# Another order for the seven products of an up-projection pair, with its releases, result split and token sums moved

## The chip, the cores and the metric

The kernel runs on one core of one Trainium2 chip. The metric is the device time of one execution in microseconds (us), the median of three runs. A core has a matrix engine, TensorE (PE, with its weight loads PEld), and three engines for elementwise work: VectorE (DVE), ScalarE (ACT) and GpSimd (POOL). SyncE (SP) issues transfers. Each engine takes its own instructions in order and waits on semaphores for the others.

## The reference

The reference is one inference step of a four-stage streaming trunk over 576 tokens of width 1024 (512 of a new stream, 64 of a running one). Each sublayer's result goes through `x <- LayerNorm(ALPHA * x + sublayer(x))`:

```
x = layer_norm(ALPHA * x + attention(x))      # chunked band attention, 16 heads
x = layer_norm(ALPHA * x + mlp_0(x))
x = layer_norm(ALPHA * x + ssm(x))            # Mamba-2 scan with convolution
x = layer_norm(ALPHA * x + mlp_1(x))
mlp(x) = square(relu(x @ W_up)) @ W_down      # 1024 -> 4096 -> 1024
```

The change touches the two MLPs alone, and in them the up-projection `square(relu(x @ W_up))`.

## The kernel before, in words

Activations lie with features on the 128 partitions and the 576 tokens in the free dimension, in two halves of 288 (T1, T2). Float32 precision comes from splitting each operand into a high part rounded for TensorE and the low rest (`xh`, `xl` for the activations, `wh`, `wl` for the weights); a product is the sum of three matmuls, high by high, high by low and low by high. A weight slab of 128x1024 is loaded by SP into `wr`, rounded on ACT into `wh` (L171), and the rest is computed on DVE into `wl` (L173).

The up-projection of an MLP has 32 tiles of 128 output features. The first four are done plainly, half by half of the tokens (`first_tiles`, matmuls L324), while the LayerNorm of the second half and the token sums run as side work between the matmuls; their relu and square are L465 and L466, the split of the result L467 and L468. The other 28 tiles of a layer go in 14 pairs (`up_pair`, matmuls L514): two weight slabs, two halves of the inner dimension and two halves of the tokens make a two-by-two block product, which seven products of blocks give in place of eight. A product is 12 matmuls of 128x288 over four blocks of 128. The names b11, b21 and b22 stand for plain activation blocks, t1 to t4 for sums of blocks. The token sums for t1 to t4 are formed once per MLP (L481, L485, L489, L496 on DVE, then `combine`: the rounding L471 on ACT and the rest L472 on DVE). The weight sums are formed per pair by four POOL operations (L187, L190, L191, L192) on the raw slabs, between the splits.

A pair holds two PSUM tiles, `ab` and `cd`, with two halves each (a, b, c, d). The results are put together in SBUF in `ut` (four rows of 288): ACT copies a finished half into it (L526, L532, L536), and DVE adds others (L524; the last add takes both halves of `cd` as 576 columns). Then ACT does relu and square over 1152 columns (L546, L547), and DVE splits the result (hh L549, hl L550). The down-projection (matmuls L294 `mm<-hh,...`) reads hh and hl; its result is added to x by L368 and L370.

The order per layer is MLP_ORDER (L68): first tiles, 3 pairs, down 0, 4 pairs, down 1, 4 pairs, down 2, 3 pairs, down 3. Each of the downs 0 to 2 is preceded by one pair that belongs to the next. Within this, a tile scheduler places the instructions on each engine's queue, so that the queues are not simply the order of the source; `W.get`, `W.load` and `W.drop` say when a weight set is formed and when its buffer may be used again.

## Time and profile before

| | |
|---|---|
| median of three runs | 1772.41 us (1769.83 to 1773.49) |
| profiled execution | 1774.35 us, its span 1772.6 us |
| PE busy | 1683.3 us, 95% |
| DVE busy | 1090.8 us, 62% |
| ACT busy | 744.1 us, 42% |
| POOL busy | 445.0 us, 25% |
| mean granted clock of PE | 0.98 |

The durations below come from the profiled execution. The span is the time from its first to its last instruction. Idle time of an engine costs something only where a chain of waits ends at PE, which is busy nearly throughout. In a timeline row the bracket gives the idle time of the engine before the instruction and what ended it; `x2` joins consecutive instructions of one form, and the duration is then that of all.

### The profile page before, as it was taken

The page shows a single profiled execution, that of the slowest core. Times are in us where ns is not written, and L with a number is a line of the kernel's source. Part 1 is how long each engine was busy: PE and PEld are TensorE (multiplying, and loading weights), DVE is VectorE, ACT ScalarE, POOL GpSimd, SP SyncE. Part 2 cuts the span into 40 slices and gives each one's busy share as a digit, 9 for nine tenths or more (in the row PEclk, how much of TensorE's full clock was granted, in tenths as well). Part 3 has the DMA queues.
Part 4 walks back from the last instruction along what each step waited for, and adds up shares of the span by engine and source line. Part 5 has one row for each costly group of instructions (what it writes and reads, how often), then busy time and mean ns, then how long its engine had stood idle before and what let it go on. Part 6 is the DMA issues. An engine that isn't in the chain of part 4 may idle for free.

```text
span 1772.6 us, 30745 instructions
## 1 busy us (share of the span) xinstructions
PE 1683.3 (95%) x12521; PEld 1592.3 (90%) x12521; DVE 1090.8 (62%) x1874; ACT 744.1 (42%) x1182; POOL 445.0 (25%) x449
## 2 busy tenths in 40 slices
PE   9999999789999999989999999999988999999995
PEld 8888888779989899989899999999877998999995
DVE  5555555885463635387776776777878636354445
ACT  5434432453241524255663563556235515243332
POOL 0000002421211312335541341334351112130211
PEclk9999999989999999999999999999988999999997
DMA  7343331113131322213432332333110313213121
GB/s 261 101 128 101 111 106 55 48 48 119 48 119 48 96 83 84 84 51 116 122 104 81 96 104 85 109 99 107 56 48 24 120 48 104 76 60 119 49 72 54
DMA packets 76924, 157.20 MB, mean 89 GB/s; under 512 B 11440, under 2 KB 40240, under 8 KB 76784
## 3 DMA queue, kind: packets, MB, share of 16 engines
q1 hardware_dynamic: 76784, 155.25, 27.5%
q8 instruction: 98, 1.61, 0.4%
q14 instruction: 42, 0.34, 0.1%
HBM read 145.80 MB, written 9.42 MB: 88 GB/s over the span
## 4 chain that ended last, share of the span: by engine, by line
PE 80%; DVE 10%; POOL 3%; ACT 3%; issue 2%; DMA 1%; SPq 0%; DVEq 0%; ACTq 0%; POOLq 0%
PE mm L294 51%; PE mm L514 12%; PE mm L324 3%; DVE wl L173 2%; PE ax L748 1%; PE mm L303 1%; ACT wh L171 1%; PE ax L1053 1%; PE ax L770 1%; PE ax L1056 1%; DVE tmp L398 1%; PE ax L719 1%; PE ax L358 1%; PE ax L1058 1%; DVE hl L550 1%
## 5 line engine op out<-in xcount | busy, mean ns | idle before, releaser
L171 ACT CAST wh<-wr 128x1024 fp32r<-128x1024 f32 (+1 forms) x279 | 279.4, 1006 | 508.0 <-PE mm L294 363.7
L173 DVE TENSOR_TENSOR wl<-wr,wh 128x1024 fp32r<-128x1024 f32 (+1 forms) x258 | 322.7, 1252 | 95.5 <-ACT wh L171 91.9
L294 PE MATMUL mm<-xh,wl 128*128 128x288 f32 x1056 | 231.6, 300 | 0.0
L294 PE MATMUL mm<-xh,wh 128*128 128x288 f32 x1056 | 230.8, 300 | 0.1
L294 PE MATMUL mm<-xl,wh 128*128 128x288 f32 x1056 | 230.8, 299 | 0.0
L294 PE MATMUL mm<-hh,wl 128*128 128x288 f32 x960 | 223.3, 298 | 0.0
L294 PE MATMUL mm<-hl,wh 128*128 128x288 f32 x960 | 223.0, 298 | 0.0
L294 PE MATMUL mm<-hh,wh 128*128 128x288 f32 x960 | 223.0, 298 | 0.0
L370 DVE TENSOR_TENSOR x<-x,mm 128x288 f32<-128x288 f32 (+1 forms) x112 | 64.7, 581 | 209.9 <-PE mm L294 198.8
L294 PEld LDWEIGHTS mm<-xl,wh 128*128 128x128 f32 x1056 | 169.3, 189 | 4.1 <-issue 3.8
L294 PEld LDWEIGHTS mm<-xh,wh 128*128 128x128 f32 x1056 | 169.7, 189 | 2.4 <-issue 1.4
L294 PEld LDWEIGHTS mm<-xh,wl 128*128 128x128 f32 x1056 | 169.6, 189 | 1.6
L294 PEld LDWEIGHTS mm<-hh,wl 128*128 128x128 f32 x960 | 161.4, 190 | 0.1
L294 PEld LDWEIGHTS mm<-hh,wh 128*128 128x128 f32 x960 | 161.3, 190 | 0.1
L294 PEld LDWEIGHTS mm<-hl,wh 128*128 128x128 f32 x960 | 161.2, 190 | 0.0
L514 PE MATMUL mm<-th,wh 128*128 128x288 f32 x336 | 106.3, 316 | 33.1 <-DVE ut L524 23.5
L514 PE MATMUL mm<-xh,wh 128*128 128x288 f32 x448 | 136.5, 305 | 0.6 <-ACT ut L532 0.6
L514 PE MATMUL mm<-xl,wh 128*128 128x288 f32 x448 | 133.5, 298 | 0.3 <-DVE xl L472 0.3
L514 PE MATMUL mm<-xh,wl 128*128 128x288 f32 x448 | 133.3, 298 | 0.0
L187 POOL TENSOR_TENSOR wr<-wr 128x512 f32<-128x512 f32 x28 | 42.0, 1500 | 342.8 <-DMA wr<-in_wts 322.4
L514 PEld LDWEIGHTS mm<-th,wh 128*128 128x128 f32 x336 | 63.7, 189 | 44.6 <-DVE ut L524 33.7
L514 PE MATMUL mm<-tl,wh 128*128 128x288 f32 x336 | 99.7, 297 | 0.0
(255 smaller groups left out, 3598.1 us busy)
## 6 DMA issues: line engine op xcount, KB each, us to landing
wr<-in_wts SPq DMA_DIRECT2D x223, 512.0 KB, 3.4
cumb<-cumd SPq DMA_DIRECT2D x32, 256.0 KB, 3.7
e<-expd SPq DMA_DIRECT2D x48, 64.0 KB, 3.4
tb<-in_rel SPq DMA_DIRECT2D x16, 160.0 KB, 3.0
out_k<-tmp SPq DMA_DIRECT2D x8, 288.0 KB, 2.3
out_v<-tmp SPq DMA_DIRECT2D x8, 288.0 KB, 2.1
tb<-in_rel SPq DMA_DIRECT2D x16, 144.0 KB, 3.0
ts<-in_rel SPq DMA_DIRECT2D x16, 144.0 KB, 2.9
```

Of the source, the lines that this page charges most:

```text
L171: S.copy(hi[:, 0:n], raw)
L173: eng.tensor_tensor(out=lo[:, 0:n], in0=raw, in1=hi[:, 0:n].bitcast(F32), op=ALU.subtract)
L187: GP.tensor_tensor(out=r2[:, lo], in0=r1[:, lo], in1=r2[:, lo], op=ALU.subtract)
L294: PE.matmul(ps[:, o:o + HALF], w, a(k)[:, t0:t0 + HALF], start=first and i == 0, stop=last and i == 2)
L303: PE.matmul(ps[:, PS0 + t0:PS0 + t0 + HALF], w, a(k)[:, t0:t0 + HALF], start=k == 0 and i == 0, stop=k == 7 and i == 2)
L324: PE.matmul(o, a, b[:, k, h * HALF:(h + 1) * HALF], start=k == 0 and i == 0, stop=k == 7 and i == 2)
L358: PE.matmul(ps[:, 96 * j:96 * j + 96], y[:, j0 + j:j0 + j + 1].to_broadcast([96, 128]), ident[0:96, 0:96], start=True, stop=True)
L370: V.tensor_tensor(out=dst, in0=dst, in1=src, op=ALU.add)
L398: V.tensor_tensor(out=acc, in0=acc, in1=sq, op=ALU.add)
L514: PE.matmul(out, a, b, start=not more and k == 0 and i == 0, stop=k == 3 and i == 2, skip_group_check=True)
L550: V.tensor_tensor(out=hl, in0=u, in1=hh.bitcast(F32), op=ALU.subtract)
L719: PE.matmul(ps[hh][:, 0:n], a[r, sl], b[r, 0:n], start=i == 0, stop=i == 2)
```

## The change

The products of a pair come in the order t3, t1, b11, t4, b21, t2, b22 in place of b11, b21, t3, t1, t2, t4, b22. The copies and adds that read a half of PSUM follow in the new order, so that the four adds lie at other places of the pair. The weights are formed in the order 2, 4, 1, 3 with one set ahead (`la=1`) and `fill()` after each release, and the weight sums are the same four per pair, in other places; the fourth set is split in two halves of 512. The rounding hh goes to ACT (`late_high`), and it and the rest hl are issued in the next pair or the next down-projection. All token sums go to POOL, as 14 operations of 128x576 per layer in place of 8 on DVE; t2 now lies in the place that t1 had, where the second half of x was, and is formed last.

```diff
             if kind == "up":
-                p += [("ups", layer, q, i, g) for i in range(i0, i1) for g in (1, 2, 4, 3)]
+                p += [("ups", layer, q, i, g) for i in range(i0, i1) for g in (2, 4, 1, 3)]
             else:
...
-            def split(self, i, raw, n=1024):
+            def split(self, i, *raws):
                 hi, lo = self.alloc()
-                S.copy(hi[:, 0:n], raw)
                 eng = GP if i in pool_lo else V
-                eng.tensor_tensor(out=lo[:, 0:n], in0=raw, in1=hi[:, 0:n].bitcast(F32), op=ALU.subtract)
+                c = 0
+                for raw in raws:
+                    sl = slice(c, c + raw.shape[-1])
+                    c = sl.stop
+                    S.copy(hi[:, sl], raw)
+                    eng.tensor_tensor(out=lo[:, sl], in0=raw, in1=hi[:, sl].bitcast(F32), op=ALU.subtract)
                 self.t[i] = (hi, lo)
...
                 lo, hi = slice(0, HALFK), slice(HALFK, 1024)
-                if p[4] == 1:
-                    self.split(i, r1)
+                if p[4] == 2:
                     GP.tensor_tensor(out=r2[:, lo], in0=r1[:, lo], in1=r2[:, lo], op=ALU.subtract)
-                elif p[4] == 2:
                     self.split(i, r2)
                     GP.tensor_tensor(out=r2[:, hi], in0=r2[:, hi], in1=r2[:, lo], op=ALU.subtract)
-                    GP.tensor_tensor(out=r1[:, lo], in0=r1[:, lo], in1=r2[:, hi], op=ALU.add)
-                    GP.tensor_tensor(out=r2[:, lo], in0=r1[:, hi], in1=r2[:, hi], op=ALU.subtract)
+                    GP.tensor_tensor(out=r2[:, lo], in0=r1[:, lo], in1=r2[:, hi], op=ALU.add)
                 elif p[4] == 4:
-                    self.split(i, r1[:, lo], HALFK)
+                    self.split(i, r2[:, lo])
+                elif p[4] == 1:
+                    self.split(i, r1)
+                    GP.tensor_tensor(out=r1[:, hi], in0=r1[:, hi], in1=r2[:, hi], op=ALU.subtract)
                 else:
-                    self.split(i, r2)
+                    self.split(i, r1[:, hi], r2[:, hi])
                     del self.raw[r], self.raw[r + 1]
...
-            def get(self, *spec):
+            def get(self, *spec, la=LA):
                 i = self.pos
...
                 self.pos += 1
-                self.load(i + LA)
+                self.load(i + la)
                 return self.t[i]
+
+            def fill(self):
+                self.load(len(plan))
...
                 def combos():
+                    for j in range(3):
+                        for kk in range(2):
+                            t, k1, k2 = sums_of(kk)
+                            sub = lambda x, y: GP.tensor_tensor(out=t, in0=x, in1=y, op=ALU.subtract)
+                            if j == 0:
+                                sub(x32[:, k2, T2], x32[:, k1, T2])
+                            elif j == 1:
+                                sub(x32[:, k1, T2], x32[:, k1, T1])
+                            else:
+                                sub(x32[:, k2, T1], x32[:, k2, T2])
+                                GP.tensor_tensor(out=t, in0=t, in1=x32[:, k1, T2], op=ALU.add)
+                                sub(t, x32[:, k1, T1])
+                            o = slice(4 * j + 2 * kk, 4 * j + 2 * kk + 2)
+                            combine(th[:, o, :], tl[:, o, :], t)
+                            yield
+
+                def last_combo():
                     for kk in range(2):
-                        t3, k1, k2 = sums_of(kk)
-                        V.tensor_tensor(out=t3, in0=x32[:, k2, T2], in1=x32[:, k1, T2], op=ALU.subtract)
-                        combine(th[:, 4 + 2 * kk:6 + 2 * kk, :], tl[:, 4 + 2 * kk:6 + 2 * kk, :], t3)
-                        yield
-                        t2, k1, k2 = sums_of(kk)
-                        V.tensor_tensor(out=t2, in0=t3, in1=x32[:, k1, T1], op=ALU.add)
-                        combine(th[:, k1, :], tl[:, k1, :], t2)
-                        yield
-                        t4, k1, k2 = sums_of(kk)
-                        V.tensor_tensor(out=t4, in0=x32[:, k2, T1], in1=t2, op=ALU.subtract)
-                        combine(th[:, 8 + 2 * kk:10 + 2 * kk, :], tl[:, 8 + 2 * kk:10 + 2 * kk, :], t4)
-                        yield
-
-                def first_combo():
-                    for kk in range(2):
-                        t1, k1, k2 = sums_of(kk)
-                        V.tensor_tensor(out=t1, in0=x32[:, k1, T2], in1=x32[:, k1, T1], op=ALU.subtract)
-                        combine(xh[:, k1, T2], xl[:, k1, T2], t1)
+                        t, k1, k2 = sums_of(kk)
+                        GP.tensor_tensor(out=t, in0=x32[:, k2, T2], in1=x32[:, k1, T2], op=ALU.subtract)
+                        GP.tensor_tensor(out=t, in0=t, in1=x32[:, k1, T1], op=ALU.add)
+                        combine(xh[:, k1, T2], xl[:, k1, T2], t)
...
                     "b22": lambda k: (xh[:, 4 + k, T2], xl[:, 4 + k, T2]),
-                    "t1": lambda k: (xh[:, k, T2], xl[:, k, T2]),
-                    "t2": lambda k: (th[:, k, :], tl[:, k, :]),
-                    "t3": lambda k: (th[:, 4 + k, :], tl[:, 4 + k, :]),
+                    "t2": lambda k: (xh[:, k, T2], xl[:, k, T2]),
+                    "t1": lambda k: (th[:, 4 + k, :], tl[:, 4 + k, :]),
+                    "t3": lambda k: (th[:, k, :], tl[:, k, :]),
                     "t4": lambda k: (th[:, 8 + k, :], tl[:, 8 + k, :]),
...
                     hpair(q, i)
-                    w1, w2, w4, w3 = (W.get("ups", layer, q, i, g) for g in (1, 2, 4, 3))
+                    get = lambda g: W.get("ups", layer, q, i, g, la=1)
                     ab, cd = mmt(), mmt()
...
                     add = lambda dst, src: V.tensor_tensor(out=dst, in0=dst, in1=src, op=ALU.add)
+                    w2 = get(2)
+                    product(d, w2, 0, "t3")
+                    S.copy(ut[:, 3, :], d)
+                    late_high()
+                    product(c, get(4), 0, "t1")
+                    add(ut[:, 3, :], c)
+                    late_low()
+                    w1 = get(1)
                     product(a, w1, 0, "b11")
                     S.copy(ut[:, 0, :], a)
+                    product(d, w2, HALFK, "t4", True)
+                    W.drop(2)
+                    W.fill()
                     product(b, w1, HALFK, "b21")
...
                     W.drop()
-                    W.load(W.pos + 2)
-                    product(d, w2, 0, "t3")
-                    S.copy(ut[:, 3, :], d)
-                    product(c, w4, 0, "t1")
-                    add(ut[:, 3, :], c)
+                    W.fill()
+                    w3 = get(3)
                     product(a, w3, HALFK, "t2", True)
...
                     add(ut[:, 3, :], a)
-                    product(d, w2, HALFK, "t4", True)
-                    W.drop(2)
-                    W.load(W.pos + 4)
                     product(c, w3, 0, "b22", True)
...
                     W.drop()
-                    W.load(W.pos + 4)
+                    W.fill()
                     u = ut.rearrange("p a b -> p (a b)")
...
                     S.activation(u, u, AF.Square)
-                    hh, hl = (x.rearrange("p a b -> p (a b)") for x in H[q, i])
-                    V.tensor_copy(hh, u)
-                    V.tensor_tensor(out=hl, in0=u, in1=hh.bitcast(F32), op=ALU.subtract)
+                    late.append((u,) + tuple(x.rearrange("p a b -> p (a b)") for x in H[q, i]))
+
+                late, lower = [], []
+
+                def late_high():
+                    while late:
+                        u, hh, hl = late.pop()
+                        S.copy(hh, u)
+                        lower.append((u, hh, hl))
+
+                def late_low():
+                    late_high()
+                    while lower:
+                        u, hh, hl = lower.pop()
+                        V.tensor_tensor(out=hl, in0=u, in1=hh.bitcast(F32), op=ALU.subtract)
...
                     side.drain()
-                    first_combo()
+                    last_combo()
...
                 def down(q):
+                    late_low()
                     hs = [H.pop((q, i)) for i in range(4)]
```

On PE, in the second stretch of pairs of the first MLP, a pair before the change passes to the next with b11 (of `ab`, mm_5376) and then t3 (of `cd`, mm_5377). Here is the end of b11 and the start of t3.

```order
L514 MATMUL mm_5376<-xl_80,wh_5247 128x288
L514 MATMUL mm_5376<-xh_79,wl_5248 128x288
L514 MATMUL mm_5377<-th_4032,wh_5281 128x288 [waits DVE_49]
L514 MATMUL mm_5377<-tl_4033,wh_5281 128x288
L514 MATMUL mm_5377<-th_4032,wl_5282 128x288
```

At the same place after the change a pair ends with the last of t2 (mm_5251) and three matmuls of b22 (mm_5252), and t3 of the next pair (mm_5393) is the first.

```order
L524 MATMUL mm_5251<-xh_79,wl_5306 128x288
L524 MATMUL mm_5252<-xh_79,wh_5305 128x288
L524 MATMUL mm_5252<-xl_80,wh_5305 128x288
L524 MATMUL mm_5252<-xh_79,wl_5306 128x288
L524 MATMUL mm_5393<-th_4032,wh_5316 128x288 [waits DVE_49]
L524 MATMUL mm_5393<-tl_4033,wh_5316 128x288
```

The matmul that waits for DVE at the boundary was preceded by the twelve of b11, which belong to the same pair; it is now preceded by the end of the pair before. The add it waits for was `ut[1:3] += cd`, and is now `ut[3] += a`.

On ACT, at the start of the first MLP, the second pair of first tiles (mm_4329) is released by L465 before the change. tmp_4342 and tmp_4358 are the sums for t4.

```order
L466 ACTIVATE tmp_4324<-tmp_4323 128x288
L171 CAST wh_4415<-wr_4044 128x512
L471 CAST th_4032<-tmp_4342 128x576
L171 CAST wh_4419<-wr_4050 128x1024
L471 CAST th_4032<-tmp_4358 128x576
L465 ACTIVATE tmp_4386<-mm_4329 128x288
L171 CAST wh_4427<-wr_4056 128x1024
L466 ACTIVATE tmp_4387<-tmp_4386 128x288
L465 ACTIVATE tmp_4392<-mm_4329 128x288
```

After the change the tile is mm_4331, the relu L472, the sums for t4 tmp_4344 and tmp_4362, and wh_4479 is the fourth weight set of the first pair.

```order
L473 ACTIVATE tmp_4326<-tmp_4325 128x288
L478 CAST th_4032<-tmp_4344 128x576
L478 CAST th_4032<-tmp_4362 128x576
L472 ACTIVATE tmp_4392<-mm_4331 128x288
L176 CAST wh_4479<-wr_4044 128x512
L473 ACTIVATE tmp_4393<-tmp_4392 128x288
L472 ACTIVATE tmp_4398<-mm_4331 128x288
L176 CAST wh_4479<-wr_4050 128x512
L473 ACTIVATE tmp_4399<-tmp_4398 128x288
L537 COPY ut_4418<-mm_4417 128x288
```

The relu that frees the second half of that tile still stands behind both casts of the sums, and now behind the first half of the fourth weight set too.

On POOL, at the same place, the queue held weight sums only.

```order
L190 TENSOR_TENSOR wr_4050<-wr_4050 128x512
L191 TENSOR_TENSOR wr_4044<-wr_4044,wr_4050 128x512
L192 TENSOR_TENSOR wr_4050<-wr_4044,wr_4050 128x512
L187 TENSOR_TENSOR wr_4425<-wr_4423,wr_4425 128x512
L190 TENSOR_TENSOR wr_4062<-wr_4062 128x512
```

After the change it holds the six operations for t4, a weight sum of the first pair (L198) and the first of the sums for t2 (tmp_4404, tmp_4409).

```order
L489 TENSOR_TENSOR tmp_4344<-x32_78 128x576
L489 TENSOR_TENSOR tmp_4362<-x32_78 128x576
L496 TENSOR_TENSOR tmp_4344<-tmp_4344,x32_78 128x576
L496 TENSOR_TENSOR tmp_4362<-tmp_4362,x32_78 128x576
L489 TENSOR_TENSOR tmp_4344<-tmp_4344,x32_78 128x576
L489 TENSOR_TENSOR tmp_4362<-tmp_4362,x32_78 128x576
L198 TENSOR_TENSOR wr_4044<-wr_4044,wr_4050 128x512
L505 TENSOR_TENSOR tmp_4404<-x32_78 128x576
L505 TENSOR_TENSOR tmp_4409<-x32_78 128x576
```

The weight sum L198 now stands behind the token sums of t4, and the sums of t2 behind it.

## Rows read from the trace of the kernel before

**Rows 1.** The page, part 1: busy us (share of the span) and instructions.

```profile
PE 1683.3 (95%) x12521; PEld 1592.3 (90%) x12521; DVE 1090.8 (62%) x1874; ACT 744.1 (42%) x1182; POOL 445.0 (25%) x449
```

**Rows 2.** Timeline, PE, a down-projection: start, duration, instruction, count.

```profile
416.83 0.43 PE L294 MATMUL mm<-hl,wh 128*128 128x288 f32 x2
...
418.43 0.43 PE L294 MATMUL mm<-hl,wh 128*128 128x288 f32 x2
```

**Rows 3.** Windows: length, busy (count) of PE, PEld, DVE, ACT, POOL, then clock, DMA share, GB/s.

```profile
371.40:416.56 45.16, 37.75 (x254) 35.73 (x253) 33.54 (x43) 24.70 (x35) 11.80 (x8) 0.92 0.30 96
467.76:519.21 51.45, 47.57 (x338) 45.12 (x337) 33.06 (x38) 26.85 (x34) 14.55 (x11) 1.00 0.28 86
...
673.05:710.12 37.07, 35.42 (x254) 33.78 (x253) 23.39 (x28) 19.74 (x25) 8.20 (x7) 1.00 0.29 90
1358.06:1403.40 45.34, 37.33 (x255) 35.58 (x253) 32.84 (x43) 24.84 (x35) 11.51 (x9) 0.92 0.30 98
```

**Rows 4.** Waits of PE: us in total, times, longest.

```profile
PE mm L514 <- DVE ut L524: 23.5, 37, 1.6
...
PE mm L514 <- ACT tmp L465: 9.5, 2, 4.8
```

**Rows 5.** Timeline, PE, from one pair to the next product t3.

```profile
493.60 0.29 PE L514 MATMUL mm<-xh,wl 128*128 128x288 f32 x1
495.46 0.40 PE L514 MATMUL mm<-th,wh 128*128 128x288 f32 x1 [1.58 <-DVE ut L524]
495.70 0.30 PE L514 MATMUL mm<-tl,wh 128*128 128x288 f32 x1
```

**Rows 6.** Timeline, PE, start of the first MLP.

```profile
372.85 0.29 PE L514 MATMUL mm<-xh,wl 128*128 128x288 f32 x1
377.88 0.61 PE L514 MATMUL mm<-th,wh 128*128 128x288 f32 x1 [4.75 <-ACT tmp L465]
```

**Rows 7.** Timeline, ACT, start of the first MLP.

```profile
367.56 0.44 ACT L466 ACTIVATE tmp<-tmp 128x288 f32<-128x288 f32 x1
...
371.30 0.62 ACT L171 CAST wh<-wr 128x512 fp32r<-128x512 f32 x1 [2.52 <-POOL wr L191]
373.75 0.67 ACT L471 CAST th<-tmp 128x576 fp32r<-128x576 f32 x1 [1.84 <-DVE tmp L485]
...
377.43 0.40 ACT L465 ACTIVATE tmp<-mm 128x288 f32<-128x288 f32 x1
```

**Rows 8.** Windows, PE after that standstill (columns of rows 3).

```profile
377.88:382.13 4.25, 4.25 (x18) 4.25 (x18) 3.47 (x8) 1.06 (x3) 1.89 (x1) 0.50 0.32 115
```

**Rows 9.** Timeline, ACT, a pair in a long stretch.

```profile
488.49 0.64 ACT L536 COPY ut<-mm 128x576 f32<-128x576 f32 x1 [2.80 <-PE mm L514]
...
492.44 2.00 ACT L171 CAST wh<-wr 128x1024 fp32r<-128x1024 f32 x2 [0.63 <-POOL wr L192]
```

**Rows 10.** Timeline, DVE, the same pair.

```profile
495.33 1.22 DVE L173 TENSOR_TENSOR wl<-wr,wh 128x1024 fp32r<-128x1024 f32 x1
497.99 0.76 DVE L549 CAST hh<-ut 128x1152 fp32r<-128x1152 f32 x1 [1.45 <-ACT ut L547]
...
503.53 0.45 DVE L524 TENSOR_TENSOR ut<-ut,mm 128x288 f32<-128x288 f32 x1 [0.94 <-ACT ut L536]
```

**Rows 11.** One line, L1095: min/median/max ns, first and last start.

```profile
L1095 POOL TENSOR_TENSOR yy<-yy,z x16: 1416/1936/1950, 863.6 to 1266.1; 128x576 f32<-128x576 f32 x16
```

**Rows 12.** Timeline, POOL, start of the first MLP.

```profile
367.99 1.75 POOL L190 TENSOR_TENSOR wr<-wr 128x512 f32<-128x512 f32 x1 [21.35 <-DVE wl L173]
...
371.22 1.51 POOL L192 TENSOR_TENSOR wr<-wr 128x512 f32<-128x512 f32 x1
```

**Rows 13.** Timeline, DVE, the same place, and L468 over the whole trace.

```profile
367.82 0.75 DVE L472 TENSOR_TENSOR tl<-tmp,th 128x576 fp32r<-128x576 f32 x1
...
370.04 3.01 DVE L468 TENSOR_TENSOR hl<-tmp,hh 128x288 fp32r<-128x288 f32 x2
...
L468 DVE TENSOR_TENSOR hl<-tmp,hh x16: 443/451/1548, 348.6 to 1366.3; 128x288 fp32r<-128x288 f32 x16
```

More of the change, by code (lines that the diff above doesn't have):

```diff
@@ L77, in slab_plan @@
             slabs.append(p)
-        elif p[4] == 1:
+        elif p[4] == 2:
             slabs += [("up", p[1], p[2], 2 * p[3] + j) for j in range(2)]
```

## The prediction, made before the result was known

> **What bounds the kernel now.** I read the page's busy times, then the stretches of the up-projection, the waits of PE and the timelines of PE, ACT, DVE and POOL around the two places where PE stands still. PE is busy for 95% of the span [rows 1], so the change can only win or lose what PE loses inside the paired tiles it rewrites. A pair is 84 matmuls. At full clock PE starts one each 0.133 us: twelve in 1.60 us [rows 2]. So a pair costs 84 x 0.133 = 11.2 us when nothing stops it. The stretches of layer 0 [rows 3] hold 3, 4, 4 and 3 pairs (the third repeats the second): 45.16, 51.45 and 37.07 us, against 33.6, 44.8 and 33.6. The losses are 11.6, 6.65 (twice) and 3.5 us, or 28.3 us; layer 1's first stretch loses 11.7 and its later ones repeat those of layer 0. Both layers lose some 57 us, which is the most that the change could give back.
>
> The waits say what the losses are [rows 4]: matmuls of L514 wait 23.5 us for the adds of L524 (37 times, at most 1.6), and 9.5 us for the relu of L465 (twice, 4.8 each). The first is the steady pair: product t3 cannot overwrite its half of PSUM until the 576-wide add has read it [rows 5]: its first matmul starts 1.86 us after the one before, not 0.13, and the second follows after 0.24 instead of 0.13. The second is the start of an MLP: PE does b11 until 372.85 and stands until 377.88 [rows 6], since the relu that frees the buffer is issued at 377.43 behind a cast that waited for POOL (371.30) and one that waited for DVE's token sum (373.75) [rows 7]. PE then runs at half clock (0.50 granted, 1.2 of 2.4 GHz) until 382.13: 18 matmuls in 4.25 us [rows 8], of which some 17 x 0.107 = 1.8 us is lost.
>
> **The change part by part.**
>
> *The steady pair.* In the new order a pair ends with twelve matmuls of t2, then only three of b22, and the next pair's t3 waits for the add of a (ut[3] += a), which stands in DVE behind ACT's broadcast copy of a (L554). Count from the start e of t2's last matmul. The copy can start when it has left PE, 0.30 after, and takes 0.64 [rows 9]: e + 0.97. The add of 288 takes 0.45 [rows 10]; with two hand-overs of about 0.05, t3 starts at e + 1.50. Three matmuls cover it until e + 0.53. So 0.97 us stand open, plus the 0.107 of the second matmul: 1.07 us. The old order hid this same release behind whole products.
>
> *The middle of the pair.* The wait of t4 and b21 is covered by seven and twelve matmuls, and I cost them at nothing. t2 waits for ut[0] += b, and nine matmuls of b22 (1.2 us) cover it; but that add is queued on DVE behind the split of w1 (1.22 [rows 10]), whose cast (1.0 each [rows 9]) cannot start before t4 ends: about 0.25 stands open, and 0.107 with it. A pair is then 11.2 + 1.07 + 0.35 = 12.6 us. Were the split of the second half of w3 late as well (t4, cast, split, POOL's L198, cast and split in a row), the pair would be 13.0; without the wait at t2 it is 12.27. Before, it is 51.45 / 4 = 12.86 in the long stretches and 37.07 / 3 = 12.36 in the last. I take 12.6: four long stretches gain 4 x 0.26 = 1.05 each, so 4.2; the two last ones lose 3 x 0.24, so 1.4 together. The sum is a gain of 2.8 us.
>
> *The late split of the result.* The rounding of hh goes from DVE to ACT: 14 casts per layer, which the trace does not show on ACT; by its rate they are as long as the square. ACT is busy 26.85 of 51.45 us in a stretch [rows 3], so there is room, and the late hl has a whole pair or the first k-blocks of a down-projection as cover: nothing. If that cover went, the copy of t3 would come late behind relu, square and cast, and t1 with it: 0.1 to 0.3 a pair, up to 8 us over 28 pairs. The fourth weight split becomes two halves of 512: one more cast and one more subtraction a pair, beside PE. SP issues the same transfers of the same slabs, and the DMA engines are busy 0.27 to 0.30 in these stretches [rows 3]: nothing.
>
> *The start of an MLP.* Here the change puts fourteen 128x576 operations on POOL where DVE did eight. The trace shows that shape on POOL only at L1095: 1.42 to 1.95 us [rows 11]. At this place POOL took 1.75 and 1.51 for 512 columns [rows 12]; the last, by 576/512, is 1.70, and I take that, as the nearest row in time. The first four (t3, t1) lie beside the LayerNorm and the first tiles. The six of t4 wait for the square that ends at 368.00 [rows 7]: 368.0 + 6 x 1.70 = 378.2. POOL's weight sum L198 follows to 379.7. ACT's queue holds the two casts of t4 and the cast of w3, which waits for L198, all ahead of the relu that frees b11's buffer. After 379.7 come 0.62 + 0.44 + 0.40 less overlap, about 1.2: b11 goes on at 380.9, where the stalled product of the kernel before started at 377.88. Thirty-six matmuls, seventeen at half clock, last until 387.5. The four sums of t2 end on POOL at 379.7 + 6.8 = 386.5; two casts and the copy that b21 waits for end at 387.5, about level. t2 ends, with its wait, at 392.8 including the last of b22. But the next t3 waits for the copy L554, and before it in ACT's queue stand five casts of the next weights; the chain is b21's end 389.5, cast of w1 to 390.8, split to 392.05, L198 to 393.4, cast 394.05, cast of the next w2 395.05, copy 395.7, add 396.2. t3 starts at 396.25: another 3.4 us of standing. Two pairs at 12.6 give an end at 421.45 against 416.56: 4.9 us lost in layer 0. Layer 1's stretch is as long [rows 3], so 4.7 there, and 9.6 together. With POOL at 1.42 the same walk gives t3 at 394.0 and 2.7 a layer; at 1.95 it gives about 398.3 and 7.
>
> The sum is 9.6 - 2.8 = +6.8 us. The profiled execution took 1774.35 us (span 1772.6), so 1781.2 there; it lies 1.94 above the median of the runs, so the forecast is 1779.2, in round figures 1779.
>
> **The rivals.**
>
> *Faster: the release at the boundary comes on time.* The place is the queue of DVE between t4's end and the boundary. If its split of w1 leaves room for ut[0] += b, and POOL does its sums at the shortest length, a pair is 12.27. The long stretches are 49.1 (4 x 2.35 = 9.4 gained), the last ones 36.8 (0.5 gained), the first stretches lose 2.7 - 0.7 = 2.0 each: -5.9 in all, 1766.5. For it: DVE loses a cast of 0.76 us per pair [rows 10], and every wait for it in the middle has seven to twelve matmuls of cover. Against it: the 1.07 at the boundary does not depend on any queue, and in the first stretch ten POOL operations stand in one chain. It decides from where the add of b ends within 1.2 us of b21's end. If the starts of both MLPs also cost no more than now, 1762.5.
>
> *About the same.* The pair at 12.4 and POOL at 1.5 or so cancel to within 3 us: 1772.
>
> *Slower still: DVE and POOL hold each other up.* Beside POOL's sums two subtractions of DVE with both inputs in SBUF took 3.01 us, which alone take 0.45 each [rows 13]: each waited for about one POOL operation. If the ten token sums in the chain at the start alternate with such operations (the tl subtraction took 0.75 there [rows 13]), each costs the chain up to 0.75: 7.5 a layer, 15 in all, so 1794. It decides only where DVE has a two-input split ready at each end of a POOL operation.
> The Trainium skill ("SBUF — State Buffer", section "Who interferes with whom") says that a DVE instruction with two SBUF inputs contends with a GpSimd instruction that reads SBUF, and that whichever issues first holds the port for its whole instruction; the 3.01 us agree with it, and it speaks against moving sums from DVE to GpSimd while DVE still has splits to do. Taken strictly it is the 1794 of this rival.
>
> **How the numbers follow.** Forecast (small loss at the starts exceeding a small gain in the pairs): 0.38. Faster by the boundary: 0.30. Same: 0.15. Held up by DVE and POOL: 0.17. About 0.2% (3.5 us) is what a measurement of this kernel can tell from no change; so faster 0.30, same 0.15, slower 0.55. The likeliest case's own range, from POOL at 1.42 to 1.95 (-4.2 to +4.4) and the pair from 12.4 to 12.8 (22 pairs x 0.2), is 1771 to 1788. For 8 in 10 the range goes from 1759, below the faster case with the starts free, to 1796, above the last rival.
>
> **What would show it.** In the changed profile the long stretches should last 50.4 us and the last ones 37.8; t3's first matmul should stand about 1 us at each boundary for the add of a, and t2's about 0.25. The first stretches should be about 50 us, with the stalled product b11 starting near 380.9 and waiting for the relu, and the next pair's t3 waiting for the add behind L554 near 396. POOL's 128x576 sums should read 1.5 to 1.9 us each. I am wrong if the long stretches fall below 49 us, if b11 goes on before 378.5, or if the sums on POOL end before PE has finished the first tiles.

## The result, and the profile after

The changed kernel took 1794.18 us (median of 4 runs, 1792.97 to 1797.36), beside 1771.12 us for the kernel before on the same chip (4 runs, 1768.34 to 1773.49): a ratio of 1.0134, 95% interval 1.0112 to 1.0155. It is slower by some 23 us, where 7 were forecast. The profiled execution took 1797.36 us with a span of 1795.6, 23.0 above the span of before. The page's first part shows that the work is the same and the share of PE smaller:

```profile
PE 1690.2 (94%) x12521; PEld 1601.5 (89%) x12521; DVE 1097.8 (61%) x1858; ACT 782.5 (44%) x1238; POOL 489.1 (27%) x477
```

The stretches of pairs, as in [rows 3] (first, second and fourth of layer 0, then the first of layer 1):

```profile
374.13:429.35 55.22, 41.75 (x254) 39.87 (x252) 38.88 (x39) 26.94 (x39) 24.07 (x17) 0.81 0.25 84
481.64:530.62 48.98, 46.52 (x338) 44.89 (x336) 32.84 (x37) 30.81 (x40) 14.14 (x11) 1.00 0.27 94
684.47:720.94 36.47, 34.83 (x254) 33.64 (x252) 23.30 (x27) 22.14 (x29) 8.88 (x7) 1.00 0.29 99
1371.88:1426.97 55.09, 41.20 (x254) 39.48 (x252) 39.09 (x39) 27.04 (x39) 24.20 (x17) 0.85 0.25 84
```

From the starts and ends of these stretches in the two traces the 23 us come out as a sum (us, both layers):

| part of the span | layer 0 | layer 1 |
|---|---|---|
| everything up to the first pair (for layer 1: from the last pair of layer 0) | +2.7 | +3.0 |
| first stretch, 3 pairs | +10.1 | +9.8 |
| the three other stretches, 11 pairs | -5.2 | -4.9 |
| the three down-projections between them | +3.2 | +3.2 |
| after the last pair | | +1.1 |

The pairs in the later stretches are shorter, as forecast. A standstill that belonged to a pair has passed to the first matmul of the down-projection (L301, and L310 for the last one of a layer; 0.8 us idle each, 1.0 from start to start), so that the two middle lines belong together: -3.6 us for 22 pairs, where -2.8 was forecast. The last down-projection of a layer has the same standstill, which is about 1 us of the +3.0 between the layers and most of the +1.1 at the end. Nearly everything else is lost around the two starts of an MLP. The waits of PE, which answer to [rows 4]:

```profile
PE mm L524 <- DVE ut L534: 20.2, 21, 2.6
...
PE mm L524 <- ACT tmp L472: 15.2, 2, 7.7
...
PE mm L524 <- ACT ut L544: 5.4, 4, 2.8
PE mm L301 <- DVE ut L534: 4.9, 6, 0.8
...
PE mm L310 <- DVE ut L534: 1.6, 2, 0.8
```

PE stands for the relu of the first tiles twice, 15.2 us where it was 9.5. The copy of b11's result (L544) holds it for 5.4 us and was no releaser of note before. The boundary of a steady pair, to be compared with [rows 5], shows the term that was right:

```profile
493.03 0.29 PE L524 MATMUL mm<-xh,wl 128*128 128x288 f32 x1
494.14 0.41 PE L524 MATMUL mm<-th,wh 128*128 128x288 f32 x1 [0.82 <-DVE ut L534]
494.38 0.29 PE L524 MATMUL mm<-tl,wh 128*128 128x288 f32 x1
```

t3 stands 0.82 us for the add, where 0.97 was forecast, and its second matmul follows after 0.24 us. A steady pair takes 12.45 to 12.50 us between the starts of its first matmuls (12.6 forecast).

At the start of the first MLP, compared with [rows 6], PE stands three times in place of once:

```profile
374.13 0.30 PE L524 MATMUL mm<-th,wh 128*128 128x288 f32 x1
...
375.59 0.29 PE L524 MATMUL mm<-th,wl 128*128 128x288 f32 x1
383.39 0.61 PE L524 MATMUL mm<-xh,wh 128*128 128x288 f32 x1 [7.51 <-ACT tmp L472]
...
391.30 0.40 PE L524 MATMUL mm<-xh,wh 128*128 128x288 f32 x1 [2.25 <-ACT ut L544]
...
402.73 0.61 PE L524 MATMUL mm<-th,wh 128*128 128x288 f32 x1 [2.63 <-DVE ut L534]
```

The granted clock (the last figure but two) after each of the three is about half, as it was after the one of [rows 8]:

```profile
383.39:388.75 5.36, 5.36 (x23) 5.36 (x24) 5.29 (x6) 2.08 (x5) 4.62 (x4) 0.54 0.60 196
391.30:395.06 3.76, 3.54 (x15) 3.19 (x16) 2.81 (x4) 0.14 (x1) 3.58 (x3) 0.56 0.00 0
402.73:408.87 6.14, 6.14 (x25) 6.14 (x26) 0.61 (x1) 3.77 (x4) 2.27 (x2) 0.50 0.18 71
```

POOL's queue there, which answers to [rows 12], shows why the first two waits are long. The first row holds the four sums for t3 and t1, then come the six for t4 (of which the first two and the last two are shown), the weight sum L198, the sums for t2, and the next pair's weight sums:

```profile
360.69 7.23 POOL L489 TENSOR_TENSOR tmp<-x 128x576 f32<-128x576 f32 x4 [13.69 <-ACT x L422]
370.95 3.41 POOL L489 TENSOR_TENSOR tmp<-x 128x576 f32<-128x576 f32 x2 [3.04 <-ACT tmp L473]
...
377.34 2.97 POOL L489 TENSOR_TENSOR tmp<-tmp,x 128x576 f32<-128x576 f32 x2
380.26 1.78 POOL L198 TENSOR_TENSOR wr<-wr 128x512 f32<-128x512 f32 x1
...
387.19 3.05 POOL L506 TENSOR_TENSOR tmp<-tmp,x 128x576 f32<-128x576 f32 x2
391.40 1.73 POOL L192 TENSOR_TENSOR wr<-wr 128x512 f32<-128x512 f32 x1 [1.16 <-DVE wl L177]
393.21 1.68 POOL L193 TENSOR_TENSOR wr<-wr 128x512 f32<-128x512 f32 x1
```

ACT's queue (compare [rows 7]) has the cast behind L198, then the relu that b11 waits for, and later the chain of casts ahead of L554:

```profile
382.08 0.62 ACT L176 CAST wh<-wr 128x512 fp32r<-128x512 f32 x1 [0.76 <-POOL wr L198]
...
382.94 0.39 ACT L472 ACTIVATE tmp<-mm 128x288 f32<-128x288 f32 x1
...
390.85 0.39 ACT L544 COPY ut<-mm 128x288 f32<-128x288 f32 x1
394.92 2.10 ACT L176 CAST wh<-wr 128x512 fp32r<-128x512 f32 x3 [3.67 <-POOL wr L193]
399.22 0.62 ACT L176 CAST wh<-wr 128x512 fp32r<-128x512 f32 x1 [2.21 <-POOL wr L198]
...
400.96 0.63 ACT L554 COPY ut<-mm 128x576 f32<-128x576 f32 x1
```

The relu is issued at 382.94 and b11 goes on at 383.39. The copy for b21 is issued at 390.85, behind the casts of t2's sums. L554, which releases t3 of the next pair, is issued at 400.96 behind a cast that waited 3.67 us for POOL's L193 and one that waited 2.21 us for L198.

### The profile page after: what moved, and what is told of

Same layout as the page of the kernel before. It is cut to its first block, busy times and chain, and to the rows that moved or that the text cites. A ratio compares the mean times of both kernels' runs of the same rounds, so it can differ in the third digit from the quotient of the medians.

```text
span 1795.6 us, 30767 instructions
## 1 busy us (share of the span) xinstructions
PE 1690.2 (94%) x12521; PEld 1601.5 (89%) x12521; DVE 1097.8 (61%) x1858; ACT 782.5 (44%) x1238; POOL 489.1 (27%) x477
## 4 chain that ended last, share of the span: by engine, by line
PE 82%; DVE 9%; ACT 4%; POOL 3%; issue 1%; DMA 1%; SPq 0%; DVEq 0%; ACTq 0%; POOLq 0%
PE mm L301 49%; PE mm L524 17%; PE mm L331 2%; PE mm L310 1%; PE ax L776 1%; DVE tmp L405 1%; PE ax L798 1%; PE ax L365 1%; PE ax L747 1%; PE ax L1081 1%; PE ax L1084 1%; PE ax L1086 1%; ACT ut L554 1%; DVE wl L177 1%; PE ax L757 1%
## 5 line engine op out<-in xcount | busy, mean ns | idle before, releaser
L176 ACT CAST wh<-wr 128x1024 fp32r<-128x1024 f32 (+1 forms) x307 | 284.7, 931 | 483.4 <-PE mm L301 360.4
L177 DVE TENSOR_TENSOR wl<-wr,wh 128x1024 fp32r<-128x1024 f32 (+1 forms) x286 | 338.2, 1186 | 75.7 <-ACT wh L176 69.1
L301 PE MATMUL mm<-xh,wl 128*128 128x288 f32 x1056 | 231.2, 299 | 0.0
L301 PE MATMUL mm<-xh,wh 128*128 128x288 f32 x1056 | 230.5, 300 | 0.1
L301 PE MATMUL mm<-xl,wh 128*128 128x288 f32 x1056 | 230.7, 299 | 0.0
L301 PE MATMUL mm<-hh,wh 128*128 128x288 f32 x960 | 223.1, 298 | 4.9 <-DVE ut L534 4.9
L301 PE MATMUL mm<-hh,wl 128*128 128x288 f32 x960 | 222.6, 297 | 0.0
L301 PE MATMUL mm<-hl,wh 128*128 128x288 f32 x960 | 222.2, 297 | 0.0
L301 PEld LDWEIGHTS mm<-xl,wh 128*128 128x128 f32 x1056 | 169.2, 189 | 4.1 <-issue 3.8
L301 PEld LDWEIGHTS mm<-xh,wh 128*128 128x128 f32 x1056 | 169.5, 189 | 2.4 <-issue 1.4
L301 PEld LDWEIGHTS mm<-xh,wl 128*128 128x128 f32 x1056 | 169.2, 189 | 1.5
L301 PEld LDWEIGHTS mm<-hh,wh 128*128 128x128 f32 x960 | 160.5, 189 | 6.4 <-DVE ut L534 6.3
L301 PEld LDWEIGHTS mm<-hh,wl 128*128 128x128 f32 x960 | 160.6, 189 | 0.1
L301 PEld LDWEIGHTS mm<-hl,wh 128*128 128x128 f32 x960 | 160.7, 189 | 0.0
L524 PE MATMUL mm<-xh,wh 128*128 128x288 f32 x448 | 138.0, 308 | 20.6 <-ACT tmp L472 15.2
L190 POOL TENSOR_TENSOR wr<-wr 128x512 f32<-128x512 f32 x28 | 38.1, 1360 | 288.2 <-DMA wr<-in_wts 288.2
L534 DVE TENSOR_TENSOR ut<-ut,mm 128x288 f32<-128x288 f32 x112 | 56.5, 525 | 85.0 <-PE mm L524 37.3
L524 PEld LDWEIGHTS mm<-xh,wh 128*128 128x128 f32 x448 | 86.4, 193 | 24.6 <-ACT tmp L472 15.6
```

The source lines that it names most:

```text
L176: S.copy(hi[:, sl], raw)
L177: eng.tensor_tensor(out=lo[:, sl], in0=raw, in1=hi[:, sl].bitcast(F32), op=ALU.subtract)
L190: GP.tensor_tensor(out=r2[:, lo], in0=r1[:, lo], in1=r2[:, lo], op=ALU.subtract)
L301: PE.matmul(ps[:, o:o + HALF], w, a(k)[:, t0:t0 + HALF], start=first and i == 0, stop=last and i == 2)
L524: PE.matmul(out, a, b, start=not more and k == 0 and i == 0, stop=k == 3 and i == 2, skip_group_check=True)
L534: add = lambda dst, src: V.tensor_tensor(out=dst, in0=dst, in1=src, op=ALU.add)
```

## The experiments

Times are compared with runs of the kernel before on the same chip, and between jobs by that ratio, since the median of before differs between jobs (1771.12 to 1774.41).

### All token sums on DVE

In the changed kernel, with nothing else touched:

```diff
-sub = lambda x, y: GP.tensor_tensor(out=t, in0=x, in1=y, op=ALU.subtract)
+sub = lambda x, y: V.tensor_tensor(out=t, in0=x, in1=y, op=ALU.subtract)
...
-GP.tensor_tensor(out=t, in0=t, in1=x32[:, k1, T2], op=ALU.add)
+V.tensor_tensor(out=t, in0=t, in1=x32[:, k1, T2], op=ALU.add)
```

The two in `last_combo` are changed likewise.

> The changed kernel with its 14 token sums per layer on DVE, nothing else changed. Theory S (the loss lies at the two MLP starts and comes from the token sums on POOL, ten of them in one chain ahead of ACT's relu and of the weight sum): the first stretch of each layer falls from 55.2 to 44-47 us, the standstill of b11 from 7.5 to under 4.5 us, and the kernel to 1770-1776 us. Rival W (the loss comes from the new places of the weight casts and weight sums, five casts ahead of the copy that frees the buffer): the first stretch stays above 52 us and the kernel above 1787 us.

Measured: 1778.01 us against 1774.10, ratio 1.0015 (1.0004 to 1.0026). Of the 1.34% of the change 1.19% are gone, some 21 of 23 us. The first stretch falls from 55.22 to 46.35 us, and the clock in it rises from 0.81 to 0.96:

```profile
373.60:419.95 46.35, 37.27 (x253) 35.24 (x252) 34.10 (x48) 26.55 (x39) 9.35 (x7) 0.96 0.30 100
472.24:521.21 48.97, 46.51 (x337) 44.84 (x336) 32.98 (x37) 30.80 (x40) 14.10 (x11) 1.00 0.28 94
```

The wait of b11 for the relu is gone. Theory S holds in its main point. The time is 2 us above its range, but the kernel before was 3 us slower in this job too; by the ratio it is 1773.8, inside the range. One standstill, that of the second pair's t3, is left and has grown:

```profile
394.24 0.40 PE L524 MATMUL mm<-th,wh 128*128 128x288 f32 x1 [4.43 <-DVE ut L534]
```

### The first four sums on POOL, the other ten on DVE

```diff
-sub = lambda x, y: GP.tensor_tensor(out=t, in0=x, in1=y, op=ALU.subtract)
+sub = lambda x, y: (V if j == 2 else GP).tensor_tensor(out=t, in0=x, in1=y, op=ALU.subtract)
```

The add of t4 and `last_combo` are on DVE.

> The changed kernel with the sums of t3 and t1 (4 operations per layer) on POOL and those of t4 and t2 (10) on DVE. If the first four lie beside the LayerNorm and the first tiles at no cost, as the prediction said: within 3 us of the kernel with all sums on DVE (1778.0). Rival (they hold the casts and DVE's subtractions there, and ACT's relu comes later): 3 to 8 us slower than that, with a standstill of b11 or t1 above 3 us.

Measured: 1777.60 us, ratio 1.0017 (1.0005 to 1.0028), the same as with all on DVE. In the whole time the four early sums cost nothing, as predicted; what costs is the chain of ten. In the one trace they are not without effect: the first tiles last 2 us longer in each layer than with all sums on DVE, and the first stretches are shorter for it (46.05 and 45.22 us against 46.35 and 47.01).

### The kernel before, with its eight sums on POOL

```diff
-V.tensor_tensor(out=t3, in0=x32[:, k2, T2], in1=x32[:, k1, T2], op=ALU.subtract)
+GP.tensor_tensor(out=t3, in0=x32[:, k2, T2], in1=x32[:, k1, T2], op=ALU.subtract)
```

The lines of t2, t4 and t1 are changed likewise.

> The kernel before with its 8 token sums per layer on POOL, nothing else changed. Theory S: the first stretch rises from 45.2 by 3 to 8 us per layer, so 1777-1787 us. Rival W: the sums cost nothing there, first stretch within 1 us of 45.2, 1769-1774 us.

Measured: 1779.33 us, ratio 1.0035 (1.0017 to 1.0052): 6 us, at the lower end of theory S's range. The first stretches are 46.53 and 47.82 us, 1.4 and 2.5 above before, and not the 3 to 8 expected. So eight sums on POOL cost under a third of what fourteen cost in the new order. What makes up the rest, the longer formula for t4 or the weight sum L198 that stands behind it, this run does not part.

### The rounding hh back on DVE, not late

```diff
-late.append((u,) + tuple(x.rearrange("p a b -> p (a b)") for x in H[q, i]))
+hh, hl = (x.rearrange("p a b -> p (a b)") for x in H[q, i])
+V.tensor_copy(hh, u)
+V.tensor_tensor(out=hl, in0=u, in1=hh.bitcast(F32), op=ALU.subtract)
```

> The changed kernel with the rounding hh back on DVE and hh and hl issued at the end of their own pair, nothing else changed. If the late split costs and brings nothing (as predicted): steady pairs stay at 12.4-12.6 us and the kernel within 4 us of 1794. If the late split is what makes the long stretches shorter than before (rival): the adds stand behind hh and hl again, pairs rise to 12.9-13.3 us and the kernel to 1804-1815 us.

Measured: 1800.43 us, ratio 1.0146 (1.0124 to 1.0168) against the change's 1.0134 (1.0112 to 1.0155). Neither expectation fits whole: by the ratio the time is 1797.0, within 4 us of 1794, but the pairs do not stay as they were. By the whole times the two kernels cannot be told apart; by the two traces nine of the 22 later pairs are 13.1 us long and the others as in the changed kernel, and the six later stretches together are 6 us longer. So in the steady pairs the late split is worth some 6 us, in place of nothing; that it brings the kernel as much is not shown.

### The boundary released by the copy alone

```diff
-add(ut[:, 3, :], a)
+add(ut[:, 3, :], ut[:, 1, :])
```

> The changed kernel, but the add that closes the boundary reads the copy of a in SBUF (ut[3] += ut[1]) in place of a in PSUM; so the next pair's t3 waits for ACT's copy alone. Theory B (the standstill at the boundary is the copy of 0.64 and the add of 0.45 in a row): it shrinks by 0.4-0.5 us, steady pairs from 12.47 to 12.0 us, 28 x 0.45 = 12.6 us less, 1780-1784 us. Rival (another wait ends last there, the weights of t3 or the add of cd): pairs above 12.3 us, kernel within 4 us of 1794.

Measured: 1783.89 us, ratio 1.0057 (1.0034 to 1.0080), 0.77% or 13.6 us less than the change. The amount is as theory B had it, the way is not. The standstill at the boundary shrinks from 0.82 to 0.33 and now waits for the copy, but t4 (the first row), which came without a wait, now waits 0.22 for an add on DVE:

```profile
494.45 0.40 PE L524 MATMUL mm<-th,wh 128*128 128x288 f32 x1 [0.22 <-DVE ut L534]
...
501.54 0.40 PE L524 MATMUL mm<-th,wh 128*128 128x288 f32 x1 [0.34 <-ACT ut L554]
```

An inner pair is 12.40 us, only 0.05 to 0.1 shorter; the first of a stretch is 0.5 shorter and the last 0.4 longer. What is gained is the wait that ends a stretch (the down-projections 0.5 us each) and 2.3 to 3.3 us in each first stretch. That the sum comes out as theory B's is luck.

### Both edits, and the next pair's weights after the copy

The fifth kernel has the sums on DVE and the boundary released by the copy.

> The changed kernel with all token sums on DVE and the boundary add reading the copy in SBUF (the edits of two earlier runs together). If they act at different places, as theory S (MLP starts) and theory B (boundaries of pairs) say: 1778.0 - 10.3 = 1767.7, so 1765-1771 us, steady pairs 12.0 to 12.4, first stretch about 46. If the shorter boundary only moves the standstill to the weights in the first stretch (rival): 1772 us or more.

Measured: 1775.48 us, ratio 1.0006 (0.9996 to 1.0015). The rival was right: of 13.6 us only 1.6 are left. The first stretches are longer than with the sums on DVE alone, 48.81 us in layer 0 and 49.06 in layer 1, where those were 46.35 and 47.01:

```profile
372.42:421.23 48.81, 38.97 (x253) 36.13 (x251) 35.25 (x48) 26.30 (x39) 9.30 (x7) 0.93 0.28 97
```

The sixth has in addition, in the first pair of an MLP, no forming of the next weights before the copy:

```diff
-                    W.fill()
+                    (q, i) != (0, LAG // 2) and W.fill()
```

(the first two of the three calls in `up_pair`).

> The same as e5, and in the first pair of each MLP the next pair's weights are formed after the copy that frees the buffer, so that ACT's queue has that copy ahead of the casts. With the sums on DVE, t3 of the second pair still stood 4.4 us at that place. Theory W (those casts, chained to POOL's weight sums, are the standstill): the wait falls below 1.5 us, and the second pair, without half clock, from 14.1 to 12.4 us; 3 to 5 us per layer, so 1758-1763 us. Rival (the wait passes to the weights of t3 and t1 themselves, which come as late as before): within 3 us of e5.

Measured: 1773.27 us, ratio 0.9991 (0.9982 to 1.0000). Again the rival: the wait for the copy falls to 0.73, and the same pair then stands for its weights, first the high part on ACT, then the low part on DVE:

```profile
387.73 0.40 PE L524 MATMUL mm<-th,wh 128*128 128x288 f32 x1 [0.73 <-ACT ut L554]
...
390.97 0.40 PE L524 MATMUL mm<-xh,wh 128*128 128x288 f32 x1 [1.37 <-ACT wh L176]
...
392.88 0.40 PE L524 MATMUL mm<-xh,wl 128*128 128x288 f32 x1 [1.37 <-DVE wl L177]
```

Later in this pair PE stands 2.40 us more for an add on DVE. The second pair took 20.3 us where the first had become 15.6. At this place the weights themselves are late, and not only the queue ahead of the copy.

### Eight sums in place of fourteen

In the fifth kernel t2 is formed once and kept in one of the two result buffers, and t4 is taken from it:

```diff
+t2s = hpool.tile([P, 4, HALF], F32, name="ut", tag="ut", bufs=2)
...
+V.tensor_tensor(out=t2, in0=t, in1=x32[:, k1, T1], op=ALU.add)
...
+V.tensor_tensor(out=t, in0=x32[:, k2, T1], in1=t2, op=ALU.subtract)
...
+combine(xh[:, k1, T2], xl[:, k1, T2], t2s[:, k1, :])
```

> The kernel e5 (sums on DVE, boundary released by the copy) with 8 token sums per layer in place of 14: t2 is formed once from t3 and kept in one of the two result buffers until its place is free, and t4 is taken from it. In e5 and e6 the standstill only moved to the next pair's weights, whose splits stand on DVE behind the sums. If DVE's work there is what sets it (theory D): 6 operations of 0.75 less are 4.5 us per layer, first stretch from 48.8 to 44-46 us, 1766-1770 us. Rival (the weight sums on POOL and casts set it, whatever DVE does): first stretch within 1.5 us of 48.8, 1773-1778 us.

Measured: 1765.34 us against 1774.05, ratio 0.9955 (0.9942 to 0.9968). This is faster than both kernels, and 8 us faster than the kernel before. It goes the way of theory D and beyond its figures: the first stretch of layer 0 is 5.5 us shorter with six operations fewer on DVE. But the edit also forms t2 early, so that no sum is left to be formed behind the first tiles; which of the two gives the gain was not parted.

```profile
372.65:415.99 43.34, 36.65 (x254) 34.97 (x252) 29.20 (x39) 24.95 (x37) 10.39 (x8) 0.96 0.32 106
```

With the early four of these eight on POOL:

> The same with the four early sums (t3 and t1) on POOL, so that DVE has only four. Theory D: DVE has another 3.0 us less per layer, but before the first tiles end, so between 0 and 3 us per layer less than e10: 1762-1770 us. Rival: as e10 or slower, since DVE's subtractions stand beside POOL's sums there.

Measured: 1766.93 us, ratio 0.9962 (0.9946 to 0.9977), not to be told from the one before, which fits both expectations. In its trace the first stretches are 42.40 and 39.04 us, the shortest of all, but the first tiles before them take 39.4 and 40.0 us, where they took 37.5 and 35.7.

### A standstill filled with idle matmuls

In the changed kernel, in the first pair of each MLP after t3:

```diff
+if (q, i) == (0, LAG // 2):
+    idle = aux(1)
+    for n in range(52):
+        PE.matmul(idle[:, 0:HALF], w2[0][:, 0:128], th[:, n % 4, :], start=n == 0, stop=n == 52 - 1)
```

`idle` is a PSUM tile that nobody reads. The scheduler then put all of t1 ahead of b11, so that it is t1 that waits.

> The changed kernel with 52 idle matmuls of 128x288 (6.9 us at full clock, into a PSUM tile that nobody reads) between t3 and the next product of the first pair of each MLP, where PE stood for 7.5 us. Theory C (what PE did before decides its clock: after the standstill 17 to 20 matmuls ran at half clock, 0.24 us apart): granted clock 1.0 there, the products after it start at the same time as without them, within 1 us, and are 1.8 us shorter, but the b21 that waits for POOL's sums gives most of it back: first stretch 53-55.5 us. Rival (half clock comes at this place whatever PE did): the same 0.5 granted after the idle matmuls.

Measured: 1790.34 us (2 runs), ratio 1.0085 (1.0068 to 1.0102), against 1.0134. By the ratios useless work made the kernel some 9 us faster. In the traces 4.0 of the 8.3 us between the two spans lie in the two first stretches; the rest lies where the two kernels issue the same instructions in the same order, at another clock in the first tiles among others, and is not shown to come of the idle matmuls. The idle matmuls, the products after them, and those after the next standstill:

```profile
373.40:380.40 7.00, 6.90 (x52) 6.67 (x51) 4.81 (x4) 2.23 (x5) 6.40 (x5) 1.00 0.00 1
382.20:386.00 3.80, 3.45 (x24) 3.22 (x24) 3.73 (x5) 0.98 (x2) 3.06 (x3) 1.00 0.70 250
```

```profile
382.28 0.41 PE L524 MATMUL mm<-th,wh 128*128 128x288 f32 x1 [1.98 <-ACT ut L537]
...
391.90 0.61 PE L524 MATMUL mm<-th,wh 128*128 128x288 f32 x1 [6.16 <-DVE ut L534]
392.30 0.44 PE L524 MATMUL mm<-tl,wh 128*128 128x288 f32 x1
```

The clock is 1.00 after the filled standstill, in both layers, so theory C holds and its rival does not: half clock there comes of what PE did before. t1 starts 10.7 us after t3 did, 1.4 later than b11 in the changed kernel and so not within the 1 us expected. After the next, unfilled standstill of 6.16 us the matmuls are 0.24 apart again. The second pair, which ran at half clock in the changed kernel, is 12.45 us instead of 15.08, and the first stretch 53.16.

## Why the prediction was off

**Right: which way, and the steady pair.** The copy and the add in a row are the wait at the boundary (0.82 against 0.97), a steady pair is 12.45 to 12.50 us against 12.6, and the later stretches with their down-projections give 3.6 us back against 2.8. The 0.25 at t2 was wrong: the trace of after shows no such wait in the steady pairs, and when the boundary came earlier it was t4, whose wait was put at nothing, that stood 0.22. Without t2's wait the prediction's own sum is 12.27, so that 12.6 came close is in part luck: the trace has two more places in a pair where a matmul follows after 0.23 to 0.24 us in place of 0.13.

**Right: what releases b11.** In the changed kernel b11 goes on 9.3 us after t3's first matmul (374.13 to 383.39), where the walk along POOL's six sums, L198 and the cast gave 9.5. The six sums took 9.4 us, 1.56 each (1.70 taken).

**Failed: the walk behind it.** The step "The start of an MLP" put 4.9 us on the first stretch; it was 10.1. The walk had t3 of the second pair 24.85 us after the first; it was 28.6 (374.13 to 402.73). Two things in it were too small.

The first is the wait for POOL. The walk put the copy ahead of b21 about level, where PE stood 2.25 us, and it led the chain to L554 from b21's end, as if the weight sums of the next pair were ready by then. By its own figures they were: the last sum of t2 15.1 us after t3's first matmul, and two weight sums of 1.3, as they take without token sums beside them, make 17.7. But POOL's L193 ended at 20.8, 3.1 later, and ACT's casts stood 3.67 for it. In the trace the last sum of t2 ends 1.0 late, L192 waits 1.16 us more for a split on DVE, and the two weight sums take 1.73 and 1.68. The split took 2.41 us, and the subtraction hl before it 1.55:

```profile
387.43 1.55 DVE L475 TENSOR_TENSOR hl<-tmp,hh 128x288 fp32r<-128x288 f32 x1
388.91 2.41 DVE L177 TENSOR_TENSOR wl<-wr,wh 128x1024 fp32r<-128x1024 f32 x1
```

With all sums on DVE the same split took 1.22 us, and L468, the hl of before, takes 0.45 alone [rows 13].

The second is the clock. It was charged once, 1.8 us, though the same walk put another standstill, of 3.4 us, at the second pair's t3. The trace has half clock after all three standstills (some 20, 12 and 25 matmuls 0.24 us apart; the windows above hold a few at full clock too). The 25 are the second pair's, 2.7 us at 0.107 each: it took 15.08 us against 12.6. What the other 32 cost was not parted, since t3 waits for ACT's queue behind them in any case. In layer 1 the second pair took 13.90 us. The run with idle matmuls shows that the second pair's part can be had back.

Together: t3 of the second pair comes 3.75 us late, the second pair takes 2.5 more than 12.6, and the third 1.1 less, since its standstill has passed to the down-projection. These are the 5.2 us that the walk missed in layer 0.

**Failed: the first tiles.** They were left out of the sum, and from their first matmul to their last they took 3.1 us more in layer 0 and 1.0 in layer 1. In layer 0 the stretch from the first matmul of the tiles to the first pair grew from 34.56 to 37.62 us, at a lower clock; the rows of after, of the kernel with all sums on DVE, of the kernel before, of the kernel before with sums on POOL, and then of the changed kernel with hh on DVE and with idle matmuls:

```profile
336.51:374.13 37.62, 32.26 (x209) 31.25 (x207) 32.38 (x49) 20.01 (x37) 19.22 (x12) 0.86 0.05 15
335.75:373.56 37.81, 32.27 (x209) 31.38 (x208) 30.77 (x54) 19.49 (x37) 9.86 (x7) 0.86 0.04 15
336.84:371.40 34.56, 29.71 (x209) 28.70 (x207) 30.62 (x53) 19.13 (x36) 9.22 (x7) 0.95 0.05 16
334.91:370.30 35.39, 29.96 (x208) 28.73 (x207) 31.81 (x49) 19.25 (x35) 15.85 (x11) 0.95 0.05 16
336.36:372.42 36.06, 29.97 (x208) 28.72 (x207) 32.69 (x49) 19.45 (x36) 18.59 (x12) 0.95 0.05 15
335.54:371.62 36.08, 29.99 (x209) 28.75 (x207) 32.73 (x49) 19.31 (x36) 18.63 (x11) 0.95 0.04 15
```

With all sums on DVE the stretch is as long as after, so the engine of the sums is not the cause in layer 0. Nor is the clock the change's alone: in the kernels of the last two rows every engine has the same instructions in the same order up to the first pair as in the changed kernel, and there the clock is 0.95 and the stretch 36.1 us. So about 1.5 of the 3.1 us are a lower clock that one execution had and another did not, and only the other 1.5 stand in every trace of the new order. In all of them PE's wait in the LayerNorm was 2.5 us or more where it was 1.83, and in the first two rows three weight sums of the first pair ran on POOL at that time in place of one. That those three are the reason was not tried.

**The rivals.** The measured time is that of the rival in which DVE and POOL hold each other up, 1794, but not by its way. It had POOL's chain stretched by 0.75 per sum, and that chain ran at 1.56, faster than assumed. It was DVE that was held, as the two DVE rows above show; even the cast hh, with one input, took 1.53 us beside the sums of t4 (at 371.53) and 0.30 without them (at 358.75). The Trainium skill ("SBUF — State Buffer", section "Who interferes with whom") has the later of two such operations wait out the whole of the other; the split of 2.41 us agrees with that, being 1.22 plus the rest of a POOL operation. Of the 23 us this explains the late weight sums, some 2 us a layer; its size was not parted from the length of POOL's chain. The rival of a boundary that comes on time was right in one thing: the add of b is no wait. Its 49.1 us are also what the long stretches read, 48.96 to 49.35, and two of them fall below the 49 that was to show the forecast wrong; but that is so only because their last standstill now counts with the down-projection. With it they are 49.9 to 50.3 us, a pair is 12.45 and not 12.27, and the starts lost more.

**Costed at nothing.** The four early sums were indeed free in the whole time. The late split was not without effect: without it, nine of the 22 pairs are 0.6 longer, some 6 us in all, so it belongs to the gain of the later stretches.

What stays open: where 1 of the 3 us between the last pair of layer 0 and the first of layer 1 went (one is the standstill at the down-projection and one lies in the first tiles; with idle matmuls the same instructions took 2.6 us less there), and why in the fifth kernel a shorter boundary does not bring its 13.6 us. That the weights of the second pair are then late is shown by the sixth; that DVE's load sets them is likely by the run with eight sums and not shown. The exact chain was not followed.

## What to carry to other kernels

Work that is moved off a busy engine onto one that is mostly idle must be followed as a chain at the place where it is due, with everything that stands behind it in that queue; POOL was busy 27% of the span and still set the time twice. Charge the price of a half clock to every long standstill of the walk, not to the first alone, and count the whole of an operation's formula: eight sums in place of fourteen gave 9 us on DVE, beside the 21 us of moving the fourteen off POOL. Before a lower clock in one trace is put down to a change, compare a second trace of the same instructions: here it was 0.86 in one and 0.95 in another. Where removing one wait moves the time little, look for the supply behind it before removing the next.

## What the runs showed that was not expected

PE's clock fell to half (1.2 of 2.4 GHz) after standstills of 7.51, 2.25 and 2.63 us within 27 us, and 52 useless matmuls in the first of them kept the granted clock at 1.00 in both layers. POOL's subtraction of 128x576 took 1.39 to 1.96 us; what sets its length was not tried:

```profile
L489 POOL TENSOR_TENSOR tmp<-x x12: 1493/1868/1958, 360.7 to 1370.8; 128x576 f32<-128x576 f32 x12
...
L489 POOL TENSOR_TENSOR tmp<-tmp,x x4: 1393/1501/1607, 377.3 to 1376.8; 128x576 f32<-128x576 f32 x4
```
